# Start addresses of the streaming tiles, half-width plain tiles and 14 weight pairs in a four-layer decoder trunk

## The chip, the cores and the metric

The kernel runs on one core of a Trainium2 chip. The metric is the device time of one execution in microseconds. The engines are named as in the profile: PE is TensorE's stream of matrix products and PEld its weight loads, DVE is VectorE, ACT is ScalarE, POOL is GpSimd, SP is SyncE.

## The reference

512 tokens of 1024 features pass through two layers. Layer 0 mixes tokens by dilated sliding-window attention, layer 1 by a gated linear recurrence (RG-LRU); each mixer is followed by a gated feed-forward block with a short causal convolution (FFN). Before and after each block stands an RMS norm, and the result is added to the residual. All is float32.

```python
for layer in range(DEPTH):                       # 2
    h = rms_norm(x, norm_mix_pre[layer])
    if layer % 2 == 0:                           # 3 groups x 8 heads of 128, window and dilation by group
        h = dilated_attention_mixer(h, attn_w_qkv[j], attn_w_o[j], rel_bias)
    else:                                        # x @ w_in, conv, gates, scan, @ w_out
        h = rglru_mixer(h, lru_w_in[j], ..., lru_w_out[j])
    x = x + rms_norm(h, norm_mix_post[layer])
    h = rms_norm(x, norm_ffn_pre[layer])
    h = conv_ffn(h, ffn_w_up[layer], ffn_conv_w[layer], ffn_conv_b[layer], ffn_w_down[layer])
    x = x + rms_norm(h, norm_ffn_post[layer])

def conv_ffn(x, w_up, conv_w, conv_b, w_down):   # w_up 1024 x 6144, w_down 3072 x 1024
    u = causal_dwconv(x @ w_up, conv_w, conv_b)
    g, v = u[..., :D_FF], u[..., D_FF:]
    return (jax.nn.gelu(g, approximate=True) * v) @ w_down
```

## The kernel before

**Split products.** Every float32 operand of a large product is split into a high part (rounded to TensorE's float32r by an ACT copy, L148) and a low part (the rest, by a DVE subtraction, L149). A product is then three passes (`PASSES`, `mm3`): high weights by high activations, high weights by low activations, low weights by high activations. The activations of a block, features on the partitions and tokens along the free axis, lie in one tile `hT` that holds both parts (`new_hT`). In most products a 128x128 piece of the weights is loaded and hT or a sum of its blocks streams past it. In the value products (L1176, L1238) and the down and output products (`acc`) it is the other way round: activations are loaded, 512 columns of weights stream.

**Weights.** `load` brings raw weights in (SP's queue), `pump` splits them into pairs of a high and a low piece of 128x512 in the pool `wp`. `HALVES` is the number of pairs, `state["live"]` counts those in use, `done` gives some back. `tick`, called after each piece of work, calls `pump`. All engine queues are written out in program order by hand (`manual_schedule`).

**Plain tiles.** `feat_tile` makes 128 output features for 512 tokens: 8 feature blocks by three passes, 24 products of 512 columns (the `L411` products that read hT). Sixteen such tiles are in the attention, twelve in the RG-LRU and eight in each FFN; one of the sixteen, and two of the eight, come as `quarters`, four pieces of 6 products put between other steps. `feat_tiles(..., True)` makes the first four tiles of the RG-LRU and of each FFN in halves of 256 tokens, all four first halves and then the second ones: 4 x 2 x 24 = 192 products of 256 columns each time.

**Seven-product steps.** Most of the FFN's up product and of the strided queries and keys goes through a scheme of Strassen's kind: a 2x2 block product by seven block products. One `chain` makes seven steps of 12 products of 256 columns (`L1040`; 4 feature blocks by three passes); there are 18 chains in each FFN and 16 in the attention. Products 1, 2 and 3 stream blocks of hT. Products 5, 6, 7 and 4 stream four token sums T, made by `token_sums`, each with a high and a low part. Between the steps stand smaller pieces: in the FFN first the quarters of two plain tiles and then down products (`rows`, 512 columns of weights), in the attention quarters of the value products, 512 columns too.

**Where the tiles lie.** The pools are laid out one after the other in each partition of the on-chip memory, so a tile's start depends on the sizes ahead of it. By *distance* I mean the start of a streaming tile less the start of the weights that are loaded for the next product while it streams, modulo 128 bytes. In the built program the pairs of `wp` start at 64 modulo 128, and `new_hT` moves its tile by `NEAR` = 16 floats (64 bytes) or by none:

| streams | attention | FFN, both layers | RG-LRU |
|---|---|---|---|
| hT (products 1, 2, 3, plain tiles) | 0 | 64 | 0 |
| sums for products 5 and 6 (in the home of the residual x) | 64 | 64 | |
| sum for product 7 (in the homes of the gains) | high part 64, low part 0 | 64 | |
| sum for product 4 (in two pairs of `wp`) | 0 | 0 | |
| split weights, past loaded hT or activations | 0 | 0 | 0 |

Of the kernel before, what the change touches and what calls it, by code (L numbers as in the profile page):

```python
# [31 lines left out]

HALVES = 16
RAW_BUFS = 3
GEN_BUFS = 32
TOE_BUFS = 2
NEAR = 16
WARM = 5
# [45 lines left out]
def kernel(  # L84
# [30 lines left out]
    gp = ctx.enter_context(tc.tile_pool(name="gp", bufs=GEN_BUFS))  # L115
    sp = ctx.enter_context(tc.tile_pool(name="sp", bufs=8))
    pp = ctx.enter_context(tc.tile_pool(name="pp", bufs=8, space=bass.MemoryType.PSUM))
# [18 lines left out]

    ident = cp.tile([P, P], F32, tag="ident", name="ident")
    make_identity(nc, ident)
    X = [cp.tile([P, 4, D], F32, tag="x_sb", name="x_sb")]

    def gain(src, layer, eng=nc.gpsimd):
        g = cp.tile([P, D], F32, tag="gain", name=nm("gain"), bufs=2)
# [134 lines left out]
    def refill():  # L277
# [14 lines left out]
        else:  # L292
# [4 lines left out]
            state["cv"] += 1  # L297

    def single(name):
        return (name[0] if isinstance(name, tuple) else name) in HALF  # L300

    def pump(limit=2):

        for _ in range(limit):
            if not pieces:
                refill()
            while pieces and pieces[0][0] is None:
                pieces.pop(0)[1]()
            if not pieces or pieces[0][0][0] >= state["dma"]:
                continue  # L310
            if state["live"] + 2 - single(pieces[0][0][1]) <= HALVES:
                key, cuts, last = pieces.pop(0)
                cuts = cuts()
                his, los = [], []
                for n, raw in enumerate(cuts):
                    hi, lo = (
                        wp.tile([P] + list(raw.shape[1:]), F32R, tag=t, name=nm("w" + t)) for t in ("hi", "lo")
                    )
# [4 lines left out]
                state["live"] += len(cuts)  # L323
# [22 lines left out]
    def take(i, j):  # L346
        while (i, j) not in units:
            before = state["live"]
            pump(1)
            assert before != state["live"], (i, j, state)  # L350
        return units[i, j]

    def done(n=2):
        state["live"] -= n
# [48 lines left out]

    def w_rows(w, r0):
        plan.append(("rows", 2, D, [(w[r0 : r0 + 256, :].rearrange("(k p) c -> p k c", p=P), 2)]))

# [144 lines left out]
    def first_roots():  # L551

        v, q = small(4), small(4)
        y = cp.tile([P, 8], F32, tag="first_y", name="first_y")[:, 0:4]
# [97 lines left out]
    def rows_run(nchunks, A, prep, seq, order, post, pre, eng):  # L652
        post_g = gain(*post, eng)
        pre_g, hT = (gain(*pre, eng), new_hT(True)) if pre is not None else (None, None)
        W, banks = {}, {}
# [14 lines left out]
        for tiles, chunks in order:  # L670
            for c in chunks:
# [9 lines left out]
                for n, part in enumerate(loop):  # L681
                    prep(seq.index(2 * c + n) + 3)
                    for t, i, kk in part:
# [7 lines left out]
                        product(t, i, k, slice(0, 512), n == 2 * nchunks, n == 1)  # L691
                        if not uses[k]:
                            done()
# [23 lines left out]
    def columns(st, n):  # L717

        ps = psum("cols")
        nc.tensor.transpose(ps[:, :n], st[:n, :P], ident[:n, :n])  # L720
        res = cp.tile([P, n], F32, tag=f"cols{n}", name=nm("cols"), bufs=4 if n == 96 else 1)
        nc.vector.tensor_copy(res, ps[:, :n])
        return res
# [3 lines left out]
    def feature_columns():  # L727
# [16 lines left out]
        la, z, sv, s2, qv = (small(8) for _ in range(5))  # L744
        c8 = cp.tile([P, KD], F32, tag="first_w", name="c8")
        twice = cp.tile([P, 3, BUCKETS], F32, tag="rb", name="twice")[:, 0, 0:8]
        nc.vector.scalar_tensor_tensor(z, lam, -1.0, lam, op0=ALU.mult, op1=ALU.min)
# [20 lines left out]
    def ffn(layer, hT, post, pre):  # L768
        ca, cc = ffn_cols[layer]
        neg = cp.tile([P, 144], F32, tag="neg", name=nm("neg"))  # L770
        nc.vector.tensor_scalar(neg[:, 0:96], ca, -1.0, None, op0=ALU.mult)
# [134 lines left out]
    def x_again():  # L906

        X[0] = cp.tile([P, 4, D], F32, tag="x_sb", name=nm("x_sb"))
        for t in range(4):
            nc.sync.dma_start(X[0][:, t], x[0, t * P : (t + 1) * P, :])  # L910
            yield 1

    def x_back():

        X[0] = cp.tile([P, 4, D], F32, tag="x_sb", name=nm("x_sb"))
        src = kept.pop()
# [5 lines left out]
    def token_sums(hT, T, first=False):  # L922

        if not first:
# [7 lines left out]
        homes = [[h[:, 0:512], h[:, 512:1024]] for h in homes]  # L932
        if first:
            homes += [[gen(F32R, "T") for _ in range(2)]]
        homes += [[wp.tile([P, 512], F32R, tag=t, name=nm("T")) for _ in range(2)] for t in ("hi", "lo")]
        state["live"] += 2
        homes = [[h.rearrange("p (k t) -> p k t", k=2) for h in hs] for hs in homes]
        yield 1 + first
# [125 lines left out]
    def seven(hT, T, begin, last, prep):  # L1064
# [44 lines left out]
        while due:  # L1109
            slot(lambda: None)  # L1110
        done(2)
        state["even"] = False
        return acc

    def attention(hT, post, pre):
        rowv = [dp.tile([8, TOE], F32, name=f"rowv{g}") for g in range(3)]

        def biases():
            rb = cp.tile([8, 3, BUCKETS], F32, tag="rb", name="rb")
            for g in range(3):  # L1120
# [342 lines left out]
        def regroup():  # L1463

            rows = dp.tile([S, 16], F32, name="strows")
            nc.gpsimd.dma_start(rows.rearrange("(a p) f -> p a f", p=P), st0.rearrange("p a s h -> p a (s h)"))
            st1 = cp.tile([P, 4, 2, 8], F32, tag="st1", name="st1")
            nc.gpsimd.dma_start(st1.rearrange("p r s h -> p (r s h)"), rows.rearrange("(u r) f -> u (r f)", r=4))
# [58 lines left out]
        state["even"] = False  # L1527
        done()
        prep(4)
# [108 lines left out]
    for c in range(4):  # L1638
        w_rows(attn_w_o[0], c * 256)
    for layer in range(2):  # L1640
        if layer:
# [6 lines left out]
            for c in range(4):  # L1648
                w_rows(lru_w_out[0], c * 256)
        for j, half in [(j, half) for j in range(12) for half in range(2)]:  # L1650
# [9 lines left out]

    first_hT = hT = new_hT()
    first_ss = [small(4) for _ in range(2)]
    roots = cp.tile([P, D], F32, tag="gain", name="roots", bufs=2)

# [6 lines left out]

    first_w.append(cp.tile([P, KD], F32, tag="first_w", name="first_w"))
    nc.scalar.dma_start(
# [66 lines left out]
```

## Time and profile before

| | |
|---|---|
| median of 3 runs | 1406.74 us (1406.62 to 1407.08) |
| profiled execution | 1406.83 us, span 1405.1 us |
| PE busy | 1395.4 us, 8741 products |
| PEld busy | 1256.1 us |
| DVE, ACT, POOL busy | 1122.2, 791.2, 225.5 us |
| mean TensorE clock granted | 0.998 |

The span runs from the first to the last instruction. A product's "mean ns" contains the time until its last result has drained, so it is longer than the time from one product's start to the next; the latter is read from pieces of the chain of waits (start in us, length in us, what, how many) or from the starts in the timeline, where neighbouring equal products are merged into one row with their count. By stages, the attention lasts until about 488 us (from 440 on its output product), the first FFN until 865, the RG-LRU until about 1020 and the second FFN to the end.

### The profile page before, as it was taken

The page shows a single profiled execution, that of the slowest core. Times are in us where ns is not written, and L with a number is a line of the kernel's source. Part 1 is how long each engine was busy: PE and PEld are TensorE (multiplying, and loading weights), DVE is VectorE, ACT ScalarE, POOL GpSimd, SP SyncE. Part 2 cuts the span into 40 slices and gives each one's busy share as a digit, 9 for nine tenths or more (in the row PEclk, how much of TensorE's full clock was granted, in tenths as well). Part 3 has the DMA queues.
Part 4 walks back from the last instruction along what each step waited for, and adds up shares of the span by engine and source line. Part 5 has one row for each costly group of instructions (what it writes and reads, how often), then busy time and mean ns, then how long its engine had stood idle before and what let it go on. Part 6 is the DMA issues. An engine that isn't in the chain of part 4 may idle for free.

```text
span 1405.1 us, 23534 instructions
## 1 busy us (share of the span) xinstructions
PE 1395.4 (99%) x8741; PEld 1256.1 (89%) x8741; DVE 1122.2 (80%) x2201; ACT 791.2 (56%) x1646; POOL 225.5 (16%) x344
## 2 busy tenths in 40 slices
PE   9999999999999999999999999999999999999998
PEld 7888999999998898999999888888898999999886
DVE  6576897888866889998888758769789999888843
ACT  7343565454536556666665645589455666666641
POOL 0341342231310102221110001000101212111000
PEclk9999999999999999999999999999999999999999
DMA  7644464656564545766654632431444777664511
GB/s 229 178 141 120 121 182 139 188 149 179 152 213 145 197 157 106 162 153 163 131 138 104 215 130 91 135 121 60 131 145 93 165 150 165 150 136 121 179 54 60
DMA packets 171883, 201.92 MB, mean 144 GB/s; under 512 B 10560, under 2 KB 141080, under 8 KB 171512
## 3 DMA queue, kind: packets, MB, share of 16 engines
q1 hardware_dynamic: 123064, 153.34, 33.9%
q0 software_dynamic: 47856, 46.02, 18.0%
q8 instruction: 69, 1.13, 0.3%
q10 hardware_dynamic: 848, 1.05, 0.2%
q14 instruction: 46, 0.38, 0.1%
HBM read 181.41 MB, written 18.96 MB: 143 GB/s over the span
## 4 chain that ended last, share of the span: by engine, by line
PE 78%; ACT 4%; DVE 4%; issue 1%; DVEq 0%; ACTq 0%
PE ps L1040 34%; PE acc L411 25%; PE ps L411 11%; PE v L1238 6%; DVE xb L1543 1%; DVE wlo L149 1%; PE O L1450 1%; PE S L1384 1%; ACT whi L148 1%; ACT sig L1564 1%; PE tr L505 1%; ACT sig L1583 0%; ACT a L1581 0%; ACT xhi L148 0%; ACT th L1582 0%
## 5 line engine op out<-in xcount | busy, mean ns | idle before, releaser
L149 DVE TENSOR_TENSOR wlo<-raw,whi 128x512 fp32r<-128x512 f32 x620 | 408.8, 686 | 110.5 <-ACT whi L148 108.4
L148 ACT ACTIVATE whi<-raw 128x512 fp32r<-128x512 f32 x620 | 367.1, 625 | 150.8 <-PE acc L411 46.6
L1040 PE MATMUL ps<-T,whi 128*128 128x256 f32 x1664 | 300.6, 281 | 0.7 <-DVE ps L1058 0.7
L411 PE MATMUL ps<-hT,whi 128*128 128x512 f32 (+1 forms) x1088 | 287.6, 353 | 0.0
L1040 PEld LDWEIGHTS ps<-T,whi 128*128 128x128 f32 x1664 | 257.8, 189 | 5.3 <-DVE ps L1058 1.3
L1040 PE MATMUL ps<-T,wlo 128*128 128x256 f32 x832 | 232.9, 280 | 0.0
L1040 PE MATMUL ps<-hT,whi 128*128 128x256 f32 x1248 | 226.0, 280 | 0.0
L411 PEld LDWEIGHTS ps<-hT,whi 128*128 128x128 f32 x1088 | 189.6, 188 | 27.7
L1040 PEld LDWEIGHTS ps<-hT,whi 128*128 128x128 f32 x1248 | 192.9, 189 | 2.6
L411 PE MATMUL ps<-hT,wlo 128*128 128x512 f32 (+1 forms) x544 | 191.5, 352 | 0.0
L1040 PE MATMUL ps<-hT,wlo 128*128 128x256 f32 x624 | 174.7, 280 | 0.0
L185 POOL DMA_DIRECT2D raw<-in_ffn_w_up_dram x72 | 92.8, 1319 | 415.7 <-DVE wlo L149 291.6
L1040 PEld LDWEIGHTS ps<-T,wlo 128*128 128x128 f32 x832 | 158.2, 190 | 0.0
L411 PE MATMUL acc<-whi,ahi 128*128 128x512 f32 x352 | 137.6, 391 | 0.0
L411 PE MATMUL acc<-whi,alo 128*128 128x512 f32 x352 | 137.2, 390 | 0.2
L411 PE MATMUL acc<-wlo,ahi 128*128 128x512 f32 x352 | 137.0, 389 | 0.0
L1040 PEld LDWEIGHTS ps<-hT,wlo 128*128 128x128 f32 x624 | 118.8, 190 | 0.0
L411 PEld LDWEIGHTS ps<-hT,wlo 128*128 128x128 f32 x544 | 102.5, 188 | 14.5
L1049 ACT ACTIVATE part<-ps 128x256 f32<-128x256 f32 x156 | 59.1, 379 | 89.3 <-PE ps L1040 86.7
L1238 PE MATMUL v<-whi,hT 128*128 128x512 f32 x320 | 106.4, 396 | 0.0
L781 DVE SCALAR_TENSOR_TENSOR u<-ps,cols,u 128x511 f32<-128x511 f32 x120 | 89.5, 747 | 5.8 <-ACT u L777 3.7
L777 ACT ACTIVATE u<-ps,cols 128x512 f32<-128x512 f32 x60 | 46.3, 775 | 64.6 <-DVE ps L1053 50.1
(206 smaller groups left out, 2144.8 us busy)
## 6 DMA issues: line engine op xcount, KB each, us to landing
raw<-in_ffn_w_up_dram SPq DMA_DIRECT2D x48, 1024.0 KB
raw<-in_attn_w_qkv_dram SPq DMA_DIRECT2D x67, 512.0 KB
raw<-in_ffn_w_up_dram POOLq DMA_DIRECT2D x72, 256.0 KB, 4.8
raw<-in_ffn_w_down_dram SPq DMA_DIRECT2D x14, 1024.0 KB
dw<-in_ffn_w_down_dram SPq DMA_DIRECT2D x40, 256.0 KB
raw<-in_lru_w_in_dram SPq DMA_DIRECT2D x8, 1024.0 KB
turned<-T POOLq DMA_DIRECT2D x26, 256.0 KB, 2.6
ft<-turned POOLq DMA_DIRECT2D x104, 64.0 KB, 4.7
```

The costliest lines, as they stand in the source:

```text
L148: nc.scalar.activation(hi, raw, AF.Copy)
L149: nc.vector.tensor_tensor(lo, raw, hi.bitcast(F32), op=ALU.subtract)
L185: nc.gpsimd.dma_start(to, src, accum_op=ALU.add)
L411: mm(dst, l[a], r[b], start=start and n == 0, stop=stop and n == 2)
L505: nc.tensor.transpose(ps[:, k * P : (k + 1) * P], xs[i][:, k * P : (k + 1) * P], ident)
L777: nc.scalar.activation(u, ps, AF.Identity, scale=own[:, j : j + 1], bias=cc[:, 48 + j : 49 + j])
L781: nc.vector.scalar_tensor_tensor(u[:, d:], ps[:, : S - d], wc, u[:, d:], op0=ALU.mult, op1=ALU.add)
L1040: mm(dst, W[wa][0][:, k, :], right[n](ha, k), start=n in (1, 5) and k == q == 0, stop=k == 3 and q == 2, skip_group_check=True,)
L1049: later(1, lambda: nc.scalar.activation(to, dst, AF.Copy))
L1238: mm(bank, hT[a][:, k, t * P : (t + 1) * P], W[b][k % 2][:, 0, :], start=(k, a, b) == (0, 0, 0), stop=(k, a, b) == (KD - 1, 1, 0),)
L1384: mm(ps[:, c], q[hh][:, c], k[hh][:, c], start=True, stop=True)
L1450: mm(po[:, c], vtile(v, r, 2 * gi + hh), pts[gi][:, r], start=gi == 0, stop=gi == 1)
```

## The change

The pools are laid out in another order and some tiles get a few floats more, so that all tiles that stream as 256 columns start at a chosen place: `new_hT` and `token_sums` move their tiles by `FAR` = 4 floats, in the attention by `NEAR` = 24. The fourth sum gets a home of its own, `last`, in the pool `sums`; the pairs of `wp` become 14. In the output products of the attention and of the RG-LRU, where no sums live, that home holds the second half of the fourth weight unit (`beside`). `feat_tile` makes its 512 tokens as two halves of 256, with the same weights loaded again, and `quarters` does so too. In the built program the pairs of `wp` start at 32 modulo 128, and the distances are:

| streams | attention | FFN, both layers | RG-LRU |
|---|---|---|---|
| hT | 64 | 112 | 112 |
| sums for products 5, 6 and 4 | 64 | 112 | |
| sum for product 7 | high part 64, low part 0 | 112 | |
| split weights, past loaded hT | 64 | | |
| split weights, past loaded activations | 0 | 0 | 0 |

```diff
-HALVES = 16
+HALVES = 14
-NEAR = 16
+FAR, NEAR, SLACK, EVEN = 4, 24, 24, 40
...
-    cp = ctx.enter_context(tc.tile_pool(name="cp", bufs=1))
-    htp = ctx.enter_context(tc.tile_pool(name="htp", bufs=1))
-    wp = ctx.enter_context(tc.tile_pool(name="wp", bufs=HALVES))
+    ip, xp, bp, n0, fp, n1, yp, htp, up_ = (pool(n) for n in ("ip", "xp", "bp", "n0", "fp", "n1", "yp", "htp", "sums"))
+    wp = pool("wp", HALVES)
     gp = ctx.enter_context(tc.tile_pool(name="gp", bufs=GEN_BUFS))
+    cp = pool("cp")
...
+    def new_last():
+        return up_.tile([P, 2 * D + EVEN], F32R, tag="sum", name=nm("last"))
...
+    def beside(key):
+        return plan[key[0]][4:] and key[1] == 1
...
-            if state["live"] + 2 - single(pieces[0][0][1]) <= HALVES:
+            spare = beside(pieces[0][0])
+            if spare and state["even"]:
+                continue
+            if spare or state["live"] + 2 - single(pieces[0][0][1]) <= HALVES:
...
-    def new_hT(near=False):
-        both = htp.tile([P, 2 * KD * S + NEAR], F32R, tag="hT", name=nm("hT"))
-        at = 0 if near else NEAR
+    def new_hT(at=FAR):
+        both = htp.tile([P, 2 * KD * S + 64], F32R, tag="hT", name=nm("hT"))
...
     def feat_tile(i, m, hT, sink):
         ps = psum()
-        feat(take(i, m), hT, ps, 0, S)
+        W = take(i, m)
+        for n in (0, 256):
+            feat(W, hT, ps, n, n + 256)
...
-        homes = cp.tile([P, 4, D], F32R, tag="x_sb", name=nm("T"))
-        homes = [homes[:, n] for n in range(4)]
-        homes += [cp.tile([P, D], F32R, tag="gain", name=nm("T"), bufs=2) for _ in range(1 if first else 2)]
...
-        homes += [[wp.tile([P, 512], F32R, tag=t, name=nm("T")) for _ in range(2)] for t in ("hi", "lo")]
-        state["live"] += 2
+        at = NEAR if first else FAR
+        large = xp.tile([P, 4 * D + SLACK], F32R, tag="x_sb", name=nm("T"))
+        last = new_last()
+        large, last = ([t[:, at + n : at + n + 512] for n in range(0, m * D, 512)] for t, m in ((large, 4), (last, 2)))
...
     def quarters(i, m, hT, finish):
...
-            for k in (2 * n, 2 * n + 1):
-                mm3(ps[0], [w[k // 4][:, k % 4, :] for w in W], [h[:, k, :] for h in hT], k == 0, k == KD - 1)
+            c = slice(n % 2 * 256, n % 2 * 256 + 256)
+            for k in range(4 * (n // 2), 4 * (n // 2) + 4):
+                mm(ps[0][:, c], W[0][k // 4][:, k % 4, :], hT[0][:, k, c], start=n == k == 0, stop=False, skip_group_check=True)
...
     def seven(hT, T, begin, last, prep):
...
-        done(2)
         state["even"] = False
...
-    first_hT = hT = new_hT()
+    first_hT = hT = new_hT(NEAR)
```

On PE, the first whole plain tile of the first FFN, half of it as before (hT_5291 is the block's activations, whi and wlo one piece of weights):

```order
L411 MATMUL ps_6140<-hT_5291,whi_5910 128x512 x2
L411 MATMUL ps_6140<-hT_5291,wlo_5911 128x512
L411 MATMUL ps_6140<-hT_5291,whi_5910 128x512 x2
L411 MATMUL ps_6140<-hT_5291,wlo_5911 128x512
L411 MATMUL ps_6140<-hT_5291,whi_5910 128x512 x2
L411 MATMUL ps_6140<-hT_5291,wlo_5911 128x512
```

And the same tile now, at the end of its first 256 tokens and the start of its second:

```order
L444 MATMUL ps_6539<-hT_5696,whi_6316 128x256 x2
L444 MATMUL ps_6539<-hT_5696,wlo_6317 128x256
L444 MATMUL ps_6539<-hT_5696,whi_6312 128x256 x2
L444 MATMUL ps_6539<-hT_5696,wlo_6313 128x256
L444 MATMUL ps_6539<-hT_5696,whi_6312 128x256 x2
L444 MATMUL ps_6539<-hT_5696,wlo_6313 128x256
```

The rows become twice as many, and the second half begins again with the weights of the first. Still on PE, product 4 of a chain of the first FFN as before, where T_5994 to T_5997 are the fourth sum in two pairs of `wp`:

```order
L1040 MATMUL ps_6379<-T_5994,whi_6471 128x256
L1040 MATMUL ps_6379<-T_5996,whi_6471 128x256
L1040 MATMUL ps_6379<-T_5994,wlo_6472 128x256
L1040 MATMUL ps_6379<-T_5994,whi_6471 128x256
L1040 MATMUL ps_6379<-T_5996,whi_6471 128x256
L1040 MATMUL ps_6379<-T_5994,wlo_6472 128x256
```

And product 4 now, of another chain there:

```order
L1082 MATMUL ps_6922<-last_6394,whi_7014 128x256 x2
L1082 MATMUL ps_6922<-last_6394,wlo_7015 128x256
L1082 MATMUL ps_6922<-last_6394,whi_7014 128x256 x2
L1082 MATMUL ps_6922<-last_6394,wlo_7015 128x256
L1082 MATMUL ps_6922<-last_6394,whi_7014 128x256 x2
L1082 MATMUL ps_6922<-last_6394,wlo_7015 128x256
```

The number of products is the same, the sum streams from its own tile. On DVE the order stays, but for the home of two weight units and the place of a few splits; at the attention's output products the fourth unit's second half is now written to `last`:

```order
L170 TENSOR_TENSOR wlo_5718<-raw_5352,whi_5717 128x512
L170 TENSOR_TENSOR wlo_5722<-raw_5352,whi_5721 128x512
L170 TENSOR_TENSOR last_5738<-raw_5352,last_5738 128x512 x2
L170 TENSOR_TENSOR alo_5746<-o_2212,ahi_5745 128x512
L170 TENSOR_TENSOR alo_5763<-o_2324,ahi_5762 128x512
```

The split stands where it stood, and only its home is another one.

More of the change, by code (lines that the diff above doesn't have):

```diff
@@ L111, with pool, lone @@
     ctx.enter_context(tc.manual_schedule())
-    cp = ctx.enter_context(tc.tile_pool(name="cp", bufs=1))
-    htp = ctx.enter_context(tc.tile_pool(name="htp", bufs=1))
-    wp = ctx.enter_context(tc.tile_pool(name="wp", bufs=HALVES))
+    def pool(name, bufs=1):
+        return ctx.enter_context(tc.tile_pool(name=name, bufs=bufs))
+    def lone(p, shape, tag):
+        return p.tile([P] + shape, F32, tag=tag, name=nm(tag))
+    ip, xp, bp, n0, fp, n1, yp, htp, up_ = (pool(n) for n in ("ip", "xp", "bp", "n0", "fp", "n1", "yp", "htp", "sums"))
+    wp = pool("wp", HALVES)
     gp = ctx.enter_context(tc.tile_pool(name="gp", bufs=GEN_BUFS))
+    cp = pool("cp")
+    col_pools = [fp, cp, cp, cp]
     sp = ctx.enter_context(tc.tile_pool(name="sp", bufs=8))
@@ L135, with new_x, next_gain @@
     mm = nc.tensor.matmul
-    ident = cp.tile([P, P], F32, tag="ident", name="ident")
+    ident = ip.tile([P, P], F32, tag="ident", name="ident")
     make_identity(nc, ident)
-    X = [cp.tile([P, 4, D], F32, tag="x_sb", name="x_sb")]
+    def new_x():
+        return xp.tile([P, 4 * D + SLACK], F32, tag="x_sb", name=nm("x_sb"))[:, : 4 * D].rearrange("p (t c) -> p t c", t=4)
+    def new_last():
+        return up_.tile([P, 2 * D + EVEN], F32R, tag="sum", name=nm("last"))
+    X = [new_x()]
+    def next_gain(dt=F32, s="gain"):
+        p = gain_pools[0]
+        gain_pools.reverse()
+        return p.tile([P, D + SLACK], dt, tag="gain", name=nm(s))[:, :D]
+    gain_pools = [n0, n1]
     def gain(src, layer, eng=nc.gpsimd):
-        g = cp.tile([P, D], F32, tag="gain", name=nm("gain"), bufs=2)
+        g = next_gain()
         row = src[layer]
@@ L314, in pump @@
                 his, los = [], []
+                if spare:
+                    t = new_last()[:, EVEN:].rearrange("p (a b o c) -> p a b o c", a=2, b=2, o=1)
                 for n, raw in enumerate(cuts):
-                    hi, lo = (
-                        wp.tile([P] + list(raw.shape[1:]), F32R, tag=t, name=nm("w" + t)) for t in ("hi", "lo")
-                    )
+                    if spare:
+                        hi, lo = t[:, 0, n], t[:, 1, n]
+                    else:
+                        hi, lo = (
+                            wp.tile([P] + list(raw.shape[1:]), F32R, tag=t, name=nm("w" + t)) for t in ("hi", "lo")
+                        )
                     split(hi, lo, raw)
@@ L322, in pump @@
                 units[key] = (his, los)
-                state["live"] += len(cuts)
+                state["live"] += len(cuts) * (not spare)
                 state["used"] += last
@@ L347, in take @@
         while (i, j) not in units:
-            before = state["live"]
+            before = len(units)
             pump(1)
-            assert before != state["live"], (i, j, state)
+            assert before != len(units), (i, j, state)
         return units[i, j]
@@ L402, in w_value, with w_rows @@
             plan.append(("value", 4, 512, [(rows[:, c0 : c0 + n].rearrange("(p k) c -> p k c", k=4), n) for c0, n in cuts]))
-    def w_rows(w, r0):
-        plan.append(("rows", 2, D, [(w[r0 : r0 + 256, :].rearrange("(k p) c -> p k c", p=P), 2)]))
+    def w_rows(w, c):
+        r0 = 256 * c
+        plan.append(("rows", 2, D, [(w[r0 : r0 + 256, :].rearrange("(k p) c -> p k c", p=P), 2)]) + (True,) * (c == 3))
     PASSES = [(0, 0), (0, 1), (1, 0)]
@@ L553, in first_roots @@
         v, q = small(4), small(4)
-        y = cp.tile([P, 8], F32, tag="first_y", name="first_y")[:, 0:4]
+        y = yp.tile([P, 16], F32, tag="first_y", name="first_y")[:, 0:4]
         nc.vector.tensor_tensor(v, first_ss[0], first_ss[1], op=ALU.add)
@@ L653, in rows_run @@
         post_g = gain(*post, eng)
-        pre_g, hT = (gain(*pre, eng), new_hT(True)) if pre is not None else (None, None)
+        pre_g, hT = (gain(*pre, eng), new_hT()) if pre is not None else (None, None)
         W, banks = {}, {}
@@ L691, in rows_run @@
                         product(t, i, k, slice(0, 512), n == 2 * nchunks, n == 1)
-                        if not uses[k]:
+                        if not uses[k] and not beside(W[k // 2][k % 2]):
                             done()
@@ L720, in columns @@
         nc.tensor.transpose(ps[:, :n], st[:n, :P], ident[:n, :n])
-        res = cp.tile([P, n], F32, tag=f"cols{n}", name=nm("cols"), bufs=4 if n == 96 else 1)
+        p = col_pools.pop(0) if n == 96 else cp
+        res = p.tile([P, n], F32, tag=f"cols{n}", name=nm("cols"), bufs=3 if n == 96 and p is cp else 1)
         nc.vector.tensor_copy(res, ps[:, :n])
@@ L744, in feature_columns @@
         la, z, sv, s2, qv = (small(8) for _ in range(5))
[L745 to L746 removed]
+        c8 = bp.tile([P, KD], F32, tag="c8", name="c8")
+        twice = yp.tile([P, KD], F32, tag="twice", name="twice")
         nc.vector.scalar_tensor_tensor(z, lam, -1.0, lam, op0=ALU.mult, op1=ALU.min)
@@ L769, in ffn @@
         ca, cc = ffn_cols[layer]
-        neg = cp.tile([P, 144], F32, tag="neg", name=nm("neg"))
+        neg = yp.tile([P, 144], F32, tag="neg", name=nm("neg"))
         nc.vector.tensor_scalar(neg[:, 0:96], ca, -1.0, None, op0=ALU.mult)
@@ L906, in x_again @@
     def x_again():
-        X[0] = cp.tile([P, 4, D], F32, tag="x_sb", name=nm("x_sb"))
+        X[0] = new_x()
         for t in range(4):
@@ L913, in x_back @@
     def x_back():
-        X[0] = cp.tile([P, 4, D], F32, tag="x_sb", name=nm("x_sb"))
+        X[0] = new_x()
         src = kept.pop()
@@ L928, in token_sums @@
             kept.append(d)
-        homes = cp.tile([P, 4, D], F32R, tag="x_sb", name=nm("T"))
-        homes = [homes[:, n] for n in range(4)]
-        homes += [cp.tile([P, D], F32R, tag="gain", name=nm("T"), bufs=2) for _ in range(1 if first else 2)]
-        homes = [[h[:, 0:512], h[:, 512:1024]] for h in homes]
+        at = NEAR if first else FAR
+        large = xp.tile([P, 4 * D + SLACK], F32R, tag="x_sb", name=nm("T"))
+        last = new_last()
+        large, last = ([t[:, at + n : at + n + 512] for n in range(0, m * D, 512)] for t, m in ((large, 4), (last, 2)))
         if first:
-            homes += [[gen(F32R, "T") for _ in range(2)]]
-        homes += [[wp.tile([P, 512], F32R, tag=t, name=nm("T")) for _ in range(2)] for t in ("hi", "lo")]
-        state["live"] += 2
-        homes = [[h.rearrange("p (k t) -> p k t", k=2) for h in hs] for hs in homes]
+            mid = [n1.tile([P, D + SLACK], F32R, tag="gain", name=nm("T"))]
+        else:
+            mid = [p.tile([P, D + SLACK], F32R, tag="gain", name=nm("T")) for p in (n0, n1)]
+        mid = [t[:, at + n : at + n + 512] for t in mid for n in (0, 512)]
+        if first:
+            mid += [gen(F32R, "T") for _ in range(2)]
+        homes = large + mid + last
+        homes = [[h.rearrange("p (k t) -> p k t", k=2) for h in homes[n : n + 2]] for n in range(0, 16, 2)]
         yield 1 + first
@@ L1118, in biases @@
         def biases():
-            rb = cp.tile([8, 3, BUCKETS], F32, tag="rb", name="rb")
+            rb = bp.tile([8, 3, BUCKETS], F32, tag="rb", name="rb")
             for g in range(3):
@@ L1670, in w_part @@
         nc.sync.dma_start(raws[i][:, k0:k1, :], plan[i][3][0][0][:, k0:k1, :])
-    first_w.append(cp.tile([P, KD], F32, tag="first_w", name="first_w"))
+    first_w.append(fp.tile([P, KD], F32, tag="first_w", name="first_w"))
     nc.scalar.dma_start(
```

11 lines of the change are left out of this document (6 added, 5 removed).

## The prediction

> **What bounds the kernel now.** I read the page first (busy time by engine), then the waits of TensorE's weight loads, then the chain that ended last, and last the timeline of TensorE.
>
> ```profile
> span 1405.1 us, 23534 instructions
> PE 1395.4 (99%) x8741; PEld 1256.1 (89%) x8741; DVE 1122.2 (80%) x2201; ACT 791.2 (56%) x1646; POOL 225.5 (16%) x344
> ...
> PEclk9999999999999999999999999999999999999999
> ```
>
> ```profile
> PEld v L1176 <- DVE wlo L149: 1.2, 3, 0.5
> PEld acc L411 <- DVE alo L149: 1.1, 2, 0.5
> ```
>
> TensorE is busy for 99% of the span and its loads hardly wait for data: the longest totals are near 1 us. So the time is the number of products times what one takes from start to start. The chain gives that without the drain that "mean ns" contains: its pieces are unbroken rows of products (start, length, count).
>
> ```profile
> 237.78 28.39 PE ps L1040 x240
> ...
> 488.28 5.66 PE ps L411 x48
> 498.52 47.21 PE ps L411 x264
> 545.72 8.16 PE ps L1040 x72
> 555.28 8.24 PE ps L1040 x72
> ...
> 593.90 9.88 PE ps L1040 x84
> 606.52 9.97 PE ps L1040 x84
> 619.23 9.82 PE ps L1040 x84
> ...
> 672.24 8.41 PE ps L1040 x72
> ...
> 769.68 8.41 PE ps L1040 x72
> ...
> 221.18 8.18 PE v L1238 x36
> 454.74 27.22 PE acc L411 x120
> 865.52 5.75 PE ps L411 x48
> ```
>
> The same 256-column product takes 113.3 ns (8.16/72), 117.6 (9.88/84), 116.8 (8.41/72), 118.3 in the attention (28.39/240) and 119.8 in the RG-LRU (5.75/48). A 512-column one takes 226.8 (27.22/120). The clock is full throughout, so it is something else. The timeline shows where the rate changes:
>
> ```profile
> 744.51 0.40 PE L1040 MATMUL ps<-hT,whi 128*128 128x256 f32 x2
> ...
> 745.92 0.40 PE L1040 MATMUL ps<-T,whi 128*128 128x256 f32 x2
> 746.15 0.28 PE L1040 MATMUL ps<-T,wlo 128*128 128x256 f32 x1
> 746.27 0.40 PE L1040 MATMUL ps<-T,whi 128*128 128x256 f32 x2
> ...
> 747.35 0.40 PE L1040 MATMUL ps<-T,whi 128*128 128x256 f32 x2
> ...
> 747.71 0.39 PE L1040 MATMUL ps<-T,whi 128*128 128x256 f32 x2
> ...
> 748.73 0.39 PE L1040 MATMUL ps<-hT,whi 128*128 128x256 f32 x2
> ```
>
> From 744.51 to 745.92 are twelve products at 117.5 ns; from 746.27 to 747.35 nine at 120.0; from 747.71 to 748.73 nine at 113.3. Nothing waits there. What changes is the tile that streams: hT at distance 64 from the weights, then the fourth token sum (homes from the weights' pool, distance 0), then the first sum (distance 64). So distance 0 makes 120; distance 64 has two lasting rates, 113.3 and 117.5, and keeps the one that it entered with. Three entries are seen: after a step at distance 0 it is 113.3 (747.71); after half tiles of hT, 512 columns at distance 64, it is 113.3 too (545.72); after half down products, 512 columns at distance 0, it is 117.6 (593.90).
>
> With 512 columns the order is turned round:
>
> ```profile
> 525.96 0.63 PE L411 MATMUL ps<-hT,whi 128*128 128x512 f32 x2
> ...
> 528.06 0.63 PE L411 MATMUL ps<-hT,whi 128*128 128x512 f32 x2
> ...
> 209.32 0.39 PE L1238 MATMUL v<-whi,hT 128*128 128x512 f32 x1
> ...
> 210.42 0.30 PEld L1040 LDWEIGHTS ps<-T,whi 128*128 128x128 f32 x2 [1.14 <-DVE ps L1058]
> ```
>
> 525.96 to 528.06 is nine FFN products at distance 64: 233.3 ns each, against 226.8 and 227.2 (8.18/36) at distance 0. The product at 209.32 had no load beside it, since the next one waited until 210.42, and it still has the 0.39 us of its kind. So I take 226.8 as the stream's own pace, and half of it, 113.4, as the floor of a 256-column product. (The Trainium skill, "TensorE: Matmul & The Clock Gate", Part 2, says that loads and the moving stream have separate read ports and that a load takes nothing from the running product. By that, distance would mean nothing and the change would only add loads; this trace disagrees, 113.3 against 120.0 ns for one shape within 3 us.)
>
> **The change part by part**, at one rate for the FFN and the RG-LRU, r, that of distance 112. No row has it. Its ends are the extremes at the other two distances: 113.3 and 120.0. By bytes it is nearest to distance 0 (16 bytes short of it), by what happens I put it with the floor: 120 belongs to the one case in which load and stream begin at the same place of the 128 bytes, and 64 shows that away from it a full-speed rate exists. I take 113.4 and keep 120 for the range.
>
> 1. FFN seven-product steps, 18 chains x 7 steps x 12 = 1512 per layer. The rows shown stand for four of 8.16 to 8.24 us, six of 9.82 to 9.97 and eight of 8.41 us in layer 0: 159.3 us for 1368 products, 116.4 ns. To 113.4: 3.0 x 1512 x 2 layers = -9.1 us. At 120: +10.9.
> 2. FFN plain tiles and fill quarters, 8 tiles x 24 = 192 products of 512 columns per layer: 233.3 becomes 2 x 113.4. 6.5 x 384 = -2.5 us; at 120, +2.6. The added loads (one for each added product) lie inside the start-to-start time, which at 256 columns has its load in it.
> 3. FFN tiles already in halves, 192 per layer: 117.9 at first (5.66/48); the 264 products after contain 144 whole ones, 33.6 us, which leaves 113.5 for 120 halves; about 115 over all. 1.6 x 384 = -0.6; at 120, +1.9.
> 4. RG-LRU halves, 192: 119.8 to 113.4 = -1.2; at 120, 0. RG-LRU whole tiles, 12 x 24 = 288, go from 226.8 (hT at distance 0 there) to 2 x 113.4: 0; at 120, +3.8.
> 5. Attention chains, 16 x 84 = 1344 products at 118.3. They mix distance 0 (all of hT and the fourth sum) with 64; now all are at 64 but the low part of the third sum. What runs between them are value products, 512 columns, which come to distance 64 as well, and after 512 columns at 64 the rate was 113.3. Small fp32 products and transposes break the rows, so 114: 4.3 x 1344 = -5.8. Ends: 113.3 (-6.7) and 117.6 (-0.9).
> 6. Attention plain tiles, 16 x 24 = 384: 227.2 to 2 x 114 = +0.3; at 117.6, +3.1.
> 7. Value products, 576: hT is the weights there and the split weights stream, now at distance 64 instead of 0. The nearest row is 233.3 against 227.2: 6.1 x 576 = +3.5; lower end 0, since that row has hT on the other side.
> 8. Fourteen pairs instead of sixteen: the fourth sum no longer takes two of the pairs, so the attention and FFN steps have 14 as before. Elsewhere two pairs fewer are made ahead; with waits of loads for wlo and alo of 2.3 us in all, 1.2 of them in the first 25 us, I cost it at 0. The cover is the remaining lead: a pair of a plain tile serves 12 products, 12 x 226.8 = 2.7 us, so 14 pairs are some 38 us ahead. If that cover were gone, each late pair would cost about one ACT and one DVE pass, 1.3 us:
>
> ```profile
> L149 DVE TENSOR_TENSOR wlo<-raw,whi 128x512 fp32r<-128x512 f32 x620 | 408.8, 686 | 110.5 <-ACT whi L148 108.4
> L148 ACT ACTIVATE whi<-raw 128x512 fp32r<-128x512 f32 x620 | 367.1, 625 | 150.8 <-PE acc L411 46.6
> 593.00:788.00 195.00, 195.00 (x1440) 185.40 (x1440) 171.05 (x275) 123.82 (x231) 30.90 (x24) 1.00 0.61 142
> ```
>
> 9. The order of DVE, ACT, POOL and SP stays but for which home two weight units go to and when a few are made: 0. DVE is next to be late: it is busy 171 of 195 us in the second FFN stretch (third figure of the last row), 90% once that stretch is 5 us shorter; still not the bound.
>
> Sum: -9.1 - 2.5 - 0.6 - 1.2 - 5.8 + 0.3 + 3.5 = -15.4 us. The profiled execution took 1406.83 us, 0.09 above the median of the runs, so 1391.
>
> **Rivals.** Steps 5 to 7 together are -2.0 in each of the first three. The FFN and RG-LRU hold 4944 products at r; their mean now, whole tiles counted as two halves, is 116.1 ns, so with the -2.0 the change stops gaining at r = 116.5 ns.
>
> A, slower: distance 112 behaves as distance 0, being only 16 bytes from it, and load and stream meet soon after the start. r = 120: +10.9 + 2.6 + 1.9 + 3.8 - 2.0 = +17.2, 1424 us. For it: 120.0 at 746.27, the nearest row by bytes. Against it: a step at that pace needs the same start. (The Trainium skill, "SBUF — State Buffer", Specifications, gives lines of 16 bytes; by that 112 is one whole line off, which fits either reading. No run so far shows it.)
>
> B, about level or a little slower: 112 has the two rates of 64, and without a step at distance 0 to bring it back it keeps the slow one after each down product. r = 117.5: 1.0 x 4.944 = +5 us, 1412. For it: 593.90. Against it: nothing but that 48 bytes lie between.
>
> C: distance is not the cause, and the steps differ by what DVE and ACT write meanwhile. Then the chains stay at 116.4 and 118.3 and only the halving counts: FFN 384 x (232.8 - 233.3) = -0.2, the other 672 whole tiles 672 x (2 x 117 - 227) = +4.7: 1411. Against it: the pace changes at the very product at which the tile does.
>
> D: the floor is lower than 113.4. (The Trainium skill, same TensorE page, "Back-to-back issue gap", has 262 cycles for 256 columns at the full clock, 109.2 ns; by that 113.4 would still contain a collision.) As a mechanism here: if all 7056 such products ran 4.1 ns under it, -28.9 more, 1362 us. Against it: the product without a load at 209.32.
>
> **How the numbers follow.** Forecast 0.64 (1384 to 1399: step 5 between its ends, step 7 between 0 and +3.5, a few us for step 8); A 0.16, B 0.09, C 0.07, D 0.04. A range of 1384 to 1424 leaves out about half of A and D, 0.12, and the forecast's own tails, some 0.06. A change under 0.2% (2.8 us) is about what a measurement of this kernel cannot tell from none; that band, 1403.9 to 1409.6, gets the near edge of B and C and the far edge of the forecast, 0.07. Faster holds nearly all of the forecast and D, 0.67; slower is A and most of B and C, 0.26.
>
> **What the profile after would show.** Step 1 right: unbroken chain pieces of the FFN's seven-product steps at 113.3 to 114 ns, with no 120.0 at the fourth sum and no 117.6 after the down products. Step 2: hT products only as 256 columns, 24 in 2.72 us. Step 5: attention pieces of 240 products near 27.3 us instead of 28.39. Step 7: value pieces of 36 near 8.4 us instead of 8.18. Step 8: no new row of loads that wait for whi or wlo. I am wrong if the FFN pieces stand at 120 (A) or 117.5 (B), or if new waits appear.

## The result, and the profile after

| | before | after |
|---|---|---|
| median of 6 runs each | 1407.03 us (1406.62 to 1408.44) | 1398.96 us (1398.78 to 1400.1) |
| ratio, 95% interval | | 0.9943 (0.993 to 0.9956) |
| profiled execution | 1406.83 us | 1398.78 us |

The change gains 8.1 us. I forecast 1391 us, a gain of 15.4. The sign came out, and so did the pace that I put on distance 112; the reason that I gave for that pace did not, as the experiments show. The size is about half: five terms of the sum were too favourable, and one of them, a cost set at nothing, turned into a wait.

The page of the kernel after, its busy times and clock:

```profile
span 1397.0 us, 25641 instructions
PE 1383.6 (99%) x9797; PEld 1285.1 (92%) x9797; DVE 1121.6 (80%) x2201; ACT 789.7 (57%) x1646; POOL 225.6 (16%) x344
...
PEclk9999999999999999999999999999999999999999
```

There are 1056 more products (and loads), and still TensorE is busy for 12 us less: the single product became cheaper. The other engines did the same work. The chain that ended last (start, length, count) shows where:

```profile
222.20 8.26 PE v L1279 x36
...
238.70 27.47 PE ps L1082 x240
...
496.16 46.30 PE ps L444 x408
542.46 8.16 PE ps L1082 x72
...
615.80 9.56 PE ps L1082 x84
...
667.81 8.20 PE ps L1082 x72
...
859.61 5.48 PE ps L444 x48
...
1147.84 9.56 PE ps L1082 x84
```

Read it against the pieces before. The long rows of the FFN's seven-product steps now take 113.3 ns (8.16/72), 113.8 (9.56/84) and 113.9 (8.20/72), where before they took 113.3, 117.6 and 116.8. The row of 408 products holds the halves and the former whole tiles of an FFN at 113.5 ns. The attention's steps went from 118.3 to 114.5 ns (27.47/240), the RG-LRU's first tiles from 119.8 to 114.2 (5.48/48). The value products went from 227.2 to 229.4 (8.26/36). New are the waits of the weight loads (total, times, longest):

```profile
PEld ps L1082 <- DVE ps L1100: 4.0, 6, 1.5
PEld ps L444 <- ACT whi L169: 1.5, 1, 1.5
...
PEld gate L444 <- ACT sig L1604: 0.8, 1, 0.8
PEld ps L444 <- DVE wlo L170: 0.6, 1, 0.6
```

The same view of before, for the two of these that existed there:

```profile
PEld ps L1040 <- DVE ps L1058: 1.3, 2, 1.1
...
PEld gate L411 <- ACT sig L1564: 0.4, 1, 0.4
```

### The profile page after: what moved, and what is told of

The parts are those of the page before. It is cut to its first block, busy times and chain, and to the rows that moved or that the text cites. A ratio compares the mean times of both kernels' runs of the same rounds, so it can differ in the third digit from the quotient of the medians.

```text
span 1397.0 us, 25641 instructions
## 1 busy us (share of the span) xinstructions
PE 1383.6 (99%) x9797; PEld 1285.1 (92%) x9797; DVE 1121.6 (80%) x2201; ACT 789.7 (57%) x1646; POOL 225.6 (16%) x344
## 4 chain that ended last, share of the span: by engine, by line
PE 82%; DVE 9%; ACT 5%; issue 2%; DMA 1%; POOL 0%; DVEq 0%; ACTq 0%; POOLq 0%
PE ps L1082 29%; PE acc L444 24%; PE ps L444 15%; PE v L1279 7%; DVE wlo L170 4%; ACT whi L169 1%; PE v L1217 1%; DVE u L816 1%; DVE xb L1583 1%; PE O L1491 1%; PE S L1425 1%; PE S L1373 1%; ACT sig L1604 1%; PE tr L537 1%; PE O L444 0%
## 5 line engine op out<-in xcount | busy, mean ns | idle before, releaser
L444 PE MATMUL ps<-hT,whi 128*128 128x256 f32 x1632 | 281.6, 277 | 1.3 <-ACT whi L169 1.3
L444 PEld LDWEIGHTS ps<-hT,whi 128*128 128x128 f32 x1632 | 247.1, 188 | 2.2 <-ACT whi L169 1.5
L444 PE MATMUL ps<-hT,wlo 128*128 128x256 f32 x816 | 225.4, 276 | 0.4 <-DVE wlo L170 0.4
L1082 PE MATMUL ps<-T,whi 128*128 128x256 f32 x1248 | 221.8, 277 | 0.0
L1082 PE MATMUL ps<-hT,whi 128*128 128x256 f32 x1248 | 220.7, 276 | 0.0
L1082 PEld LDWEIGHTS ps<-T,whi 128*128 128x128 f32 x1248 | 191.5, 188 | 3.0
L1082 PEld LDWEIGHTS ps<-hT,whi 128*128 128x128 f32 x1248 | 190.0, 188 | 2.0
L1082 PE MATMUL ps<-T,wlo 128*128 128x256 f32 x624 | 172.5, 276 | 0.0
L1082 PE MATMUL ps<-hT,wlo 128*128 128x256 f32 x624 | 172.1, 276 | 0.0
L444 PEld LDWEIGHTS ps<-hT,wlo 128*128 128x128 f32 x816 | 153.4, 188 | 0.6 <-DVE wlo L170 0.6
L444 PE MATMUL acc<-whi,ahi 128*128 128x512 f32 x336 | 131.4, 391 | 0.0
L444 PE MATMUL acc<-whi,alo 128*128 128x512 f32 x336 | 131.0, 390 | 0.2
L1082 PEld LDWEIGHTS ps<-T,wlo 128*128 128x128 f32 x624 | 117.2, 188 | 0.0
L1082 PEld LDWEIGHTS ps<-hT,wlo 128*128 128x128 f32 x624 | 117.2, 188 | 0.0
```

The costliest lines, as they stand in the source:

```text
L444: mm(dst, l[a], r[b], start=start and n == 0, stop=stop and n == 2)
L1082: mm(dst, W[wa][0][:, k, :], right[n](ha, k), start=n in (1, 5) and k == q == 0, stop=k == 3 and q == 2, skip_group_check=True,)
```

## The experiments

Three questions: does the distance set the pace, and how (eight kernels that differ only in FAR and NEAR); what is halving worth by itself (two); is the new wait at the RG-LRU's start the price of 14 pairs (two). Distance is as defined above. In the changed kernel it is 4 FAR - 32 for the FFN and the RG-LRU and 4 NEAR - 32 for the attention, modulo 128; the value products, where hT is loaded, move with NEAR too, to 32 - 4 NEAR. Kernels with one execution are compared with one execution of before beside them, 1407.56 us for the first four and 1407.12 us for the last four; the effects there are 4 to 35 us.

**Distance 0 everywhere.**

```diff
-FAR, NEAR, SLACK, EVEN = 4, 24, 24, 40
+FAR, NEAR, SLACK, EVEN = 8, 8, 24, 40
```

> The changed kernel with FAR = NEAR = 8 floats: every tile that streams as 256 columns keeps one distance everywhere, but that distance is 0. Theory P (the gain is the distance itself: the load and the stream that run side by side must not start at the same place of the 128 bytes): the seven-product steps of the FFN go from 113.9 to 120 ns, the attention's too, and the whole takes about 1436 us (7056 products, 5 to 6 ns more each, less 1 us for the value products). Rival U (what counts is that the distance never changes from step to step, whatever it is): as the changed kernel, 1399 us, pieces of 84 FFN products at 9.6 us.

Measured: 1432.22 us, 33 above the change with the same instructions. Chain pieces, first of the attention, then of the FFN:

```profile
242.75 28.45 PE ps L1082 x240
...
641.59 10.08 PE ps L1082 x84
```

118.5 and 120.0 ns, near theory P's 120 and 1436 us. The start addresses alone move the whole kernel; that the steps differ by what else is written meanwhile (C) is out.

**Distance 64 in the FFN, 112 in the attention.**

```diff
-FAR, NEAR, SLACK, EVEN = 4, 24, 24, 40
+FAR, NEAR, SLACK, EVEN = 24, 4, 24, 40
```

> The changed kernel with FAR = 24 (FFN and RG-LRU at distance 64) and NEAR = 4 (attention at 112): the two places swap their distances. Theory P with the two lasting rates that the kernel before showed at 64: FFN pieces stand at 117.6 ns after the down products (84 products in 9.9 us), at 113.4 after the quarters; about 2 x 5 us more in the two FFNs. In the attention, 112 brings 113.9 ns in pieces of 240 (27.3 us, against 27.47 at 64). In all 1405 to 1412 us. Rival U: 1399 us. Rival E (64 has only one lasting rate when nothing at distance 0 lies between): FFN pieces of 84 at 9.6 us, 1399 us.

Measured: 1411.17 us; B's price for a change that gets stuck in the slow rate was 1412. Chain pieces:

```profile
239.74 27.56 PE ps L1082 x240
...
545.43 8.16 PE ps L1082 x72
...
631.35 9.89 PE ps L1082 x84
```

The two rates of 64 are back in the FFN, 113.3 ns before the down products and 117.7 behind them, though the weights now start at 32 modulo 128 and not at 64. Distance 0, too, takes 120.0 ns with the weights at 64 (before) and at 32 (the kernel above). So, as far as these two distances show, it is the distance that counts, and not the place of the weights. In the attention 112 (114.8 ns) is no better than 64 (114.5). Rivals U and E are out.

**Distance 96 everywhere.**

```diff
-FAR, NEAR, SLACK, EVEN = 4, 24, 24, 40
+FAR, NEAR, SLACK, EVEN = 0, 0, 24, 40
```

> The changed kernel with FAR = NEAR = 0: distance 96 everywhere. Theory P says only that it is not 120 (no common start); the rate lies between 113.4 and 117.6 ns and the time between 1396 and 1420 us. If the rate is set by how near the distance is to 0 (rival N: nearness), 96 is farther from 0 than 112 and must be at least as fast as 112: 1399 us or less. Rival U: 1399 us.

Measured: 1438.32 us.

```profile
243.97 28.75 PE ps L1082 x240
...
632.73 10.08 PE ps L1082 x84
```

119.8 and 120.0 ns, as bad as a common start, with 32 bytes between. Uniform addresses are not what helps, since here they are as uniform as in the change; and my reason for the floor at 112, that it is away from the common start, does not hold. Theory P and rival N both expected a shorter time than this. Nor is it the start of the stream alone: hT starts at 0 modulo 128 here and in the FFNs before, where it took 113.3 and 117.5 ns.

**Distance 32 everywhere.**

```diff
-FAR, NEAR, SLACK, EVEN = 4, 24, 24, 40
+FAR, NEAR, SLACK, EVEN = 16, 16, 24, 40
```

> The changed kernel with FAR = NEAR = 16: distance 32 everywhere, as far above 0 as 96 lies below it. Rival N (nearness alone, no matter on which side): as distance 96. Theory P with a sign (the stream runs through its bytes faster than the load, so that a stream that starts behind the load meets it and one that starts ahead runs away, or the other way round): 32 and 96 differ, one of them near 113.9 ns, the other nearer 117 to 120; the slower of the two takes 1415 to 1436 us. Rival U: 1399 us.

Measured: 1424.36 us.

```profile
242.89 28.18 PE ps L1082 x240
...
639.55 9.97 PE ps L1082 x84
```

117.4 and 118.7 ns: between the extremes, which none of the three theories said.

**Distances 16 and 48**, to see whether the pace falls or rises along the way from 0 to 64.

```diff
-FAR, NEAR, SLACK, EVEN = 4, 24, 24, 40
+FAR, NEAR, SLACK, EVEN = 12, 12, 24, 40
```

> The changed kernel with FAR = NEAR = 12: distance 16 everywhere. So far the FFN's 256-column products take 119.4 ns at 0, 118.2 at 32, 115.9 at 64, 120.0 at 96, 113.9 at 112. Theory G (a falling slope from 0 upwards to a sharp rise between 64 and 96): 118.8 ns, 1428 us. Rival M (the neighbours of 0 on both sides are good, as 112 is): 113.9 ns, 1400 us.

Measured: 1412.31 us.

```profile
241.02 27.44 PE ps L1082 x240
...
634.28 9.80 PE ps L1082 x84
```

```diff
-FAR, NEAR, SLACK, EVEN = 4, 24, 24, 40
+FAR, NEAR, SLACK, EVEN = 20, 20, 24, 40
```

> The changed kernel with FAR = NEAR = 20: distance 48 everywhere. Theory G: between 118.2 (at 32) and 115.9 (at 64), about 117 ns, 1415 to 1420 us. Rival M (steps of 16 bytes alternate or are irregular): anything from 113.9 to 120, told apart from G if it lies under 115.9 or over 118.2 ns.

Measured: 1429.44 us.

```profile
242.45 28.58 PE ps L1082 x240
...
641.63 10.01 PE ps L1082 x84
```

At 16 it is 114.3 and 116.7 ns, at 48 it is 119.1 and 119.2. Going from 0 by 16 bytes the FFN's pieces are 120.0, 116.7, 118.7, 119.2 and then the two rates of 64: neither a slope in either direction nor a simple distance from the nearest common start. Theory G missed both times; of M only the irregular steps are left, since the good neighbour of 0 on this side (113.9 ns) did not come in the FFN.

**Distances 104 and 120**, half a 16-byte step on either side of 112 (the attention stays at 64 in the first and goes to 56 in the second).

```diff
-FAR, NEAR, SLACK, EVEN = 4, 24, 24, 40
+FAR, NEAR, SLACK, EVEN = 2, 24, 24, 40
```

> The changed kernel with FAR = 2: distance 104 in the FFN and the RG-LRU, half way between the worst (96, 120.0 ns) and the best (112, 113.9 ns) that were measured, attention as changed. Theory L (the memory is read in pieces of 16 bytes, and 104 lies in the same piece as 96): 120 ns, FFN pieces of 84 at 10.08 us, about 1427 us. Rival T (the rate follows the distance by less than 16 bytes): about 117 ns, 9.8 us, 1412 us.

Measured: 1436.21 us.

```profile
239.08 27.47 PE ps L1082 x240
...
635.37 10.11 PE ps L1082 x84
```

```diff
-FAR, NEAR, SLACK, EVEN = 4, 24, 24, 40
+FAR, NEAR, SLACK, EVEN = 6, 22, 24, 40
```

> The changed kernel with FAR = 6 and NEAR = 22: distance 120 in the FFN and the RG-LRU, 56 in the attention. Theory L: 120 lies in the piece of 112, 113.9 ns, FFN pieces of 84 at 9.56 us; 56 in that of 48. Rival T: between 113.9 and 119.4, about 116.5 ns, 9.8 us, about 1410 us.

Measured: 1442.5 us, the slowest of all.

```profile
243.94 28.80 PE ps L1082 x240
...
633.69 10.16 PE ps L1082 x84
```

In the first the attention's piece is that of the change to the last digit, the FFN's takes 120.4 ns instead of 113.8; in the second 120.0 and 121.0. Theory L fits the first rate and not the second, T neither. So 112 is no broad dip: 8 bytes to either side, off the 16-byte grid, the gain is gone. But the grid is not enough either, since 0, 48 and 96 lie on it. No theory that I set up fits all the distances.

**The change with whole plain tiles**: the new addresses without the halving.

```diff
-        W = take(i, m)
-        for n in (0, 256):
-            feat(W, hT, ps, n, n + 256)
+        feat(take(i, m), hT, ps, 0, S)
```

and `quarters` as before.

> The changed kernel with the plain tiles and the quarters whole again (1056 products of 512 columns in place of 2112 of 256), all addresses as changed. If a whole product at 112 and 64 goes at its own pace of 226.8 ns, halving is worth nothing and this takes 1397 to 1400 us. If it collides as the whole FFN products did before (233.3 ns at distance 64), the 384 of the attention and the 672 at distance 112 lose 5 to 6 ns each against two halves: 1403 to 1405 us. My sum gave halving 2.5 us in the FFN alone.

Measured: 1403.24 us (1402.82 to 1404.21, 7 runs; before 1407.09, 18 runs), ratio 0.9974 (0.9964 to 0.9985).

```profile
497.83 46.94 PE ps L444 x264
...
618.17 9.56 PE ps L1077 x84
```

The same work took 46.30 us as 408 halves. With 120 halves at 113.8 ns, 144 whole products are left with 231.1 ns each. Halving is worth 1403.24 - 1398.96 = 4.3 us at the new addresses, and the addresses with the 14 pairs 3.9.

**Before with halved plain tiles**, the same edit at the old addresses.

```diff
-        feat(take(i, m), hT, ps, 0, S)
+        W = take(i, m)
+        for n in (0, 256):
+            feat(W, hT, ps, n, n + 256)
```

and `quarters` as after.

> The kernel before with the plain tiles and quarters in halves and nothing else. Theory P: FFN tiles (distance 64) gain 384 x (233.3 - 2 x 115.5) = 0.9 us; those of the attention and the RG-LRU (distance 0) lose 672 x (2 x 119.5 - 227) = 8.1 us: 1413 to 1415 us. Rival: halves help by themselves (finer steps, fewer stalls): 1407 us or less.

Measured: 1413.24 us (1412.61 to 1415.03, 4 runs), ratio 1.0046 (1.0032 to 1.006): 6.2 us lost. Pieces of an FFN and of the RG-LRU:

```profile
503.81 46.25 PE ps L411 x408
...
939.44 46.07 PE ps L411 x384
```

Where hT is at distance 0, the halves take 120.0 ns each (46.07/384), against 113.4 for half a whole product there; in the FFN, at 64, they take 113.4 (46.25/408), against 116.7. The same edit costs 6 us at one set of addresses and gains 4 at another.

**Before with 14 pairs** from the first FFN's down products to the RG-LRU's first four tiles, the time in which the lead for the RG-LRU is built up.

```diff
-            if state["live"] + 2 - single(pieces[0][0][1]) <= HALVES:
+            if state["live"] + 2 - single(pieces[0][0][1]) <= state["cap"]:
...
+            state["cap"] = 14 if pre is not None else HALVES
...
         feat_tiles(2, hT, lambda j, ps: conv(ps, j), True)
+        state["cap"] = HALVES
```

> The kernel before, allowed only 14 of its 16 weight pairs from the first FFN's last down products to the RG-LRU's first four tiles. Theory S (the new wait at the RG-LRU's start in the changed kernel, 1.5 us for whi and 0.6 for wlo, comes from the two pairs that are missing): the same wait of about 2 us appears there, 1408.5 to 1410 us. Rival F (the wait comes from TensorE being faster and ACT and DVE not): no wait there, 1407 us.

Measured: 1408.6 us (1408.27 to 1412.93, 10 runs), ratio 1.0013 (1.0004 to 1.0022). The two new waits of after appear in it, with the same lengths, at the old addresses:

```profile
PEld ps L411 <- ACT whi L148: 1.5, 1, 1.5
...
PEld ps L411 <- DVE wlo L149: 0.6, 1, 0.6
```

So the two pairs fewer make this wait, not the addresses or the halves.

**The change with a spare home for the RG-LRU.** The tile `last` is idle from the first FFN's last chain until the RG-LRU's output products. This kernel splits the weights of the fourth of the RG-LRU's first four tiles into it.

```diff
-                    t = new_last()[:, EVEN:].rearrange("p (a b o c) -> p a b o c", a=2, b=2, o=1)
+                    t = new_last()[:, EVEN:].rearrange("p (a b o c) -> p a b o c", a=2, b=2, o=cuts[0].shape[1])
...
-                        done()
+                        if not beside((ids[j // 2], j % 2)):
+                            done()
...
-        plan.append((kind, KD, 256, srcs))
+        plan.append((kind, KD, 256, srcs) + (True,) * spare)
...
-                    w_cols(w_in, n * 256 + (D if kind == "b" else 0))
+                    w_cols(w_in, n * 256 + (D if kind == "b" else 0), spare=(kind, n) == ("x", 1))
```

> The changed kernel, and the weights of the RG-LRU's fourth half tile are split into the home of the fourth sum, which is free then, so that two more pairs stand ready at the RG-LRU's start. Theory S: the wait of 2.1 us at 870 us goes, 1396.5 to 1397.5 us, a gain of 1.3 to 2.2 us on the changed kernel. Rival F: the wait stays or moves a tile on, 1398.5 to 1399.5 us.

Measured: 1397.1 us (1396.07 to 1397.89, 5 runs), ratio 0.9929 (0.9917 to 0.9942). Its chain at the RG-LRU's start, and its waits of weight loads:

```profile
861.98 5.48 PE ps L444 x48
...
868.33 2.78 PE ps L444 x24
871.11 0.88 PE tr L537 x8
```

```profile
PEld ps L1083 <- DVE ps L1101: 5.6, 7, 2.1
```

The row of products goes on through 870 us, and no load waits for whi or wlo there. The RG-LRU's stage is 3.3 us shorter than in the change. Of that, 1.9 us are seen in the medians; the profiled execution, the longest of its five, lost 2.4 us in the attention, where the loads wait 3.9 us for DVE's additions and not 2.2; what brings that is not known. It has the lowest median of all kernels here, but its interval against before overlaps that of the change.

## Why the prediction was right, and where it was too large

I summed the starts to starts of each kind of product over each stage of the two profiled executions; the column "measured" is after less before.

| step | predicted us | measured us |
|---|---|---|
| 1 FFN seven-product steps | -9.1 | -5.7 |
| 2, 3 FFN plain tiles, quarters, halves | -3.1 | -2.8 |
| down products between the steps | none | +1.0 |
| 4 RG-LRU | -1.2 | +1.6 (with 8) |
| 5 attention steps | -5.8 | -4.0 |
| 6 attention plain tiles | +0.3 | +1.1 |
| 7 value products | +3.5 | +0.9 |
| 8 fourteen pairs | 0 | in 4 |
| sum | -15.4 | -7.9 (executions: -8.05) |

**Step 1**, the rate: right as a value, wrong in its reason. I took 113.4 ns and the pieces show 113.8 to 113.9, which is 0.45 x 3024 = 1.4 us of the 3.4 missing. The timeline of after shows that these rows are not even:

```profile
667.65 0.39 PE L1082 MATMUL ps<-hT,whi 128*128 128x256 f32 x2
...
668.71 0.39 PE L1082 MATMUL ps<-hT,whi 128*128 128x256 f32 x2
...
669.73 0.39 PE L1082 MATMUL ps<-T,whi 128*128 128x256 f32 x2
```

Behind a group of down products, the first nine products take 117.8 ns (667.65 to 668.71) and the next nine 113.3 (668.71 to 669.73). I had expected no 117.6 behind the down products; it is there, but here it ends after nine products, where at distance 64 it lasts. So a step of 12 that stands alone between down products still takes 116.7 ns (1.40/12), against 117.5 before. Such a step and the down products behind it, after:

```profile
665.02 1.40 PE ps L1082 x12
666.42 1.39 PE acc L444 x6
```

And before:

```profile
669.47 1.41 PE ps L1040 x12
670.88 1.36 PE acc L411 x6
```

Most of the rest is a wait that the faster products uncover. The timeline of after, in the first FFN:

```profile
595.29 0.28 PE L1082 MATMUL ps<-hT,wlo 128*128 128x256 f32 x1
595.50 0.42 DVE L1100 TENSOR_TENSOR ps<-ps,part 128x256 f32<-128x256 f32 x1
...
595.98 0.50 PE L1082 MATMUL ps<-last,whi 128*128 128x256 f32 x2 [0.41 <-DVE ps L1100]
```

Product 4 would start 0.11 us after the last hT product, but the addition on DVE (595.50 to 595.92) that frees its bank comes late. In each FFN two such waits make 0.9 us together by the loads, where before has none; by the products' starts it is 1.0 us against 0.2. Of the eight kernels above, which run the same order, the seven whose FFN steps take 116.7 ns or more throughout have no such wait in the first FFN. Step 9 named DVE as next to be late and gave it no price.

The reason I gave, that 112 belongs with the floor because it is away from the common start, is refuted: 96, 104 and 120 are away from it too and take 120.0 to 121.0 ns. That 112 is near the floor all the same was luck: a forecast that lands for a wrong reason must be counted as a guess between the two ends, and the 0.16 that I gave to A was too little for what I knew.

**Steps 2 and 3** came out: 0.3 us apart. The whole-tile kernel shows the halving at work.

**Steps 4 and 8**: the failed step is "I cost it at 0". Here is the place in the timeline of after:

```profile
868.58 1.04 PE L537 MATMUL tr<-ident,xs 128*128 128x128 f32 x8
869.22 1.09 ACT L541 ACTIVATE hT<-tr 128x512 fp32r<-128x512 f32 x2 [1.56 <-PE tr L537]
870.20 3.23 ACT L169 ACTIVATE whi<-raw 128x512 fp32r<-128x512 f32 x6
...
870.88 0.50 PE L444 MATMUL ps<-hT,whi 128*128 128x256 f32 x2 [1.25 <-ACT whi L169]
...
871.79 0.39 PE L444 MATMUL ps<-hT,wlo 128*128 128x256 f32 x1 [0.41 <-DVE wlo L170]
```

The cover that I named was a lead of 38 us, 14 pairs by 2.7 us. That counts every pair as if it stood ready for a plain tile. At the end of the down products it does not: followed through the kernel's code, all 14 pairs are in use there, eight by the last down products and six by the RG-LRU's first three tiles (two pairs each). Then `hold`, a switch of the kernel that stops `pump` while the norms of the last tokens run, stops all splitting. The down products give their eight pairs back, but nothing is split into them, and the RG-LRU starts with the weights of its fourth tile unsplit. Before, 16 pairs were eight for the down products and eight for all four tiles. So the fourth tile's weights are split only when `hold` ends, behind the copies of hT on ACT (870.20 in the timeline), and TensorE waits for them. The price that I gave for a lost cover, one ACT and one DVE pass or 1.3 us for a late pair, was met by 2.1 us in sum (1.5 and 0.6). That the pairs are the cause is shown by before with 14 pairs, which has the wait, and by the spare home, which has not; how `hold` comes into it is read from the code and the timeline, and no run varied it. The rest of step 4 stands: the products by themselves gained 0.3 us including 0.7 of these waits, so 1.0 without them, near the 1.2 forecast. The wait for `sig` before the gate products grew by 0.4.

**Step 5**: the rows of 240 took 114.5 ns for 114. The 624 products outside of these rows gained 2.0 ns each by their starts, where I had put 4.3, and the loads' waits for DVE's additions grew from 1.3 to 2.2 us. **Step 6**, at +1.1, lies between its two ends. **Step 7**: the nearest row (233.3) had hT on the other side, and the side matters: at the same distance the value products take 229.4 ns. The lower end of 0 was the better one.

**The down products**, which keep distance 0, were not in the sum and became 0.8 ns dearer each in the mean. The loss sits at the start of a group: the six behind a step of 256 columns take 231.7 ns each (1.39/6), and took 226.7 (1.36/6, in the pieces under step 1). I have no cause for that.

**Rivals.** A and D did not happen; B's lasting slow rate is real and belongs to 64 (1411.17 us against its 1412); at 112 it lasts nine products. C is out. The Trainium skill, "TensorE: Matmul & The Clock Gate", Part 2, has separate read ports for loads and stream, so that a load takes nothing from the running product. The runs disagree: with the same instructions the FFN's piece of 84 takes 9.56 us in the change and 9.80 to 10.16 in the eight kernels, by start addresses alone.

## What to carry to other kernels

When TensorE is busy for 99% of the span and its clock is full, compare the start-to-start time of equal products over the whole kernel: two paces for one shape are worth a search over the start addresses of the streaming tile and of the weights, and the search has to be run, since no rule found here says which distance is good. Halving a product's columns is priced only together with that address. A buffer lead counted in pairs holds only while pairs are filled as they come free; where the program stops filling them for a while, count what stands ready at the moment that it stops.

## What the runs showed of the hardware

For a float32r product of 256 columns past freshly loaded weights, at a granted clock of 0.997 to 0.999, in ns from start to start (FFN: piece of 84, at 64 also one of 72; attention: piece of 240, with small products of other kinds between the pieces):

| distance, bytes | 0 | 16 | 32 | 48 | 56 | 64 | 96 | 104 | 112 | 120 |
|---|---|---|---|---|---|---|---|---|---|---|
| FFN | 120.0 | 116.7 | 118.7 | 119.2 | | 113.3 and 117.7 | 120.0 | 120.4 | 113.8 (117.8, then 113.3) | 121.0 |
| attention | 118.5 | 114.3 | 117.4 | 119.1 | 120.0 | 114.5 | 119.8 | | 114.8 | |

Both rows have their lowest figures at 16, 64 and 112 and high ones at 0, 48, 96 and where the distance is no multiple of 16; at 32 they lie between. The low ones lie 48 bytes apart, and so do 0, 48 and 96. That was noticed only after the runs, 80 was not tried, and it is no explanation; why 112 comes to the floor stays open. So does why 64 has two lasting rates, and why 16 comes to the floor in the attention but not in the FFN.

The Trainium skill, "SBUF — State Buffer", Specifications, says that each crossing into a new line of 16 bytes costs something. 56, 104 and 120, at 120.0 to 121.0 ns, agree with a cost for starts inside a line, but 0, 48 and 96 are whole lines off and cost nearly as much, so by these runs lines alone are not the cause.
